# Turning the rows of a layer norm back with identity matmuls, outside the norms

## The chip, the cores and the metric

The kernel runs on one core of one Trainium2 chip. The time is what the device measures for one execution of the whole program, in microseconds (us). The engines are named as in the profile: PE (TensorE) multiplies matrices, PEld is its loading of weights, DVE (VectorE) and ACT (ScalarE) work element by element, POOL (GpSimd) issues the gathers, SP (SyncE) issues most loads.

## The reference

One decoder block on 512 tokens of width 2048, all in float32:

```
for l in range(DEPTH):                                            # DEPTH = 1
    h = hybrid_mixer(x, w_in[l], ..., w_out[l])                   # mLSTM and forgetting attention
    x = layer_norm(DN_ALPHA * x + h, ln_w[l, 0], ln_b[l, 0])      # norm 0
    h = memory_cross_attention(x, mem, w_xq[l], w_xkv[l], w_xo[l])
    x = layer_norm(DN_ALPHA * x + h, ln_w[l, 1], ln_b[l, 1])      # norm 1
    h = peer_ffn(x, peer_wq[l], peer_sub_keys[l], peer_u[l], peer_v[l])
    x = layer_norm(DN_ALPHA * x + h, ln_w[l, 2], ln_b[l, 2])
```

`layer_norm` takes off the mean over the 2048 columns, divides by the root of the variance plus 1e-5, multiplies by `w` and adds `b`. `peer_ffn` scores the tokens against sub-keys, selects 16 experts for each of 8 heads, multiplies the tokens by the experts' rows of `peer_u`, and sums rows of `peer_v` by the results.

## The kernel before, in words

**Matmuls in two parts.** Every large matmul is made of three matmuls in fp32r: a tile is split into a high part (rounded to fp32r by a copy on ACT, L157 for activations, L194 for weights) and a low part (the difference, on DVE, L158 and L199). High by high, high by low and low by high are summed. Weights come as 1 MB tiles `raw`; each is cast and subtracted into a **ring** tile of 4096 columns, half for the high and half for the low part. With one tile in the ring a raw tile is split in two shares that use the tile's halves in turn; `add_ring` adds a second tile, and from then on a whole raw tile is one share and the counter `ring["n"]` picks the tile:

```
L188  ring["n"] += 1
L190  t = ring["tiles"][ring["n"] % len(ring["tiles"])]
```

The first share after the second tile is added (before the output projections of blocks 1 to 3, at 2484 us) goes to the new tile, the next to the old one, `ring0`. `group_as` (L242) runs such shares with the activations as weights of PE and 512 columns moving: L262 and L263 for the high shares, L270 for the low one.

**Rows and columns.** The 512 tokens are four blocks of 128 rows. An object of class `Ends` holds one set of blocks: `e` block 0, `e1` block 1 (one block each), `e2` blocks 2 and 3. Each goes through a residual (L785: old rows times alpha plus the group's bank, for four groups of 512 columns), norm 0 (L802), the cross attention, a second residual and norm 1. A norm holds its rows in `r[t][g]` (block t, group g). Group by group it normalises the rows (L818 on ACT or L820 on DVE), turns them to columns by transposes (L828, with the 128x128 identity `ident` moving), applies scale and shift on the columns into `f` (L836 on ACT, L838 on DVE), and splits `f` into the high and low parts that the next matmuls take (L157, L158). Then it turns `f` back to rows: four transposes for each block and group into one bank (L852), a copy into `r[t][g]` on ACT (L853), and for the norms with `dst` a store to `x2d` in DRAM (L855). These rows are the next residual's old rows, and in DRAM the rows of `peer_ffn` and of the last residual. Over the six norms there are 32 such pairs of block and group.

**Order.** Python generators are mixed by hand (`mix`, `take`, `behind`), and the tile framework's scheduler orders each engine's instructions. Banks of PSUM: five `mm`, and three small ones in rotation (`sm_bank`: one `s1`, two `s2`). From norm 1 of `e2` on, products with the experts' rows for later use (`next_a`, L1388 to L1397, evacuated by L1402) run while the selection of experts for blocks 2 and 3 runs on DVE (L946 to L1009), and their bank `pa` is tagged `s2` too. Then the **gate build**: the chosen indices and gates are transposed (L1441), one-hot tiles are made (`o1` by L1455 with three buffers, `o0` by L1458), scaled on ACT (L1461), multiplied (L1462) and copied out (L1467), with a `next_a` after every second step.

## Time and profile before

| what | value |
|---|---|
| time, median of 3 runs | 4514.42 us (4506.16 to 4519.79) |
| the profiled execution's own time | 4513.31 us |
| its span, and TensorE clock granted | 4511.6 us, 0.991 |
| instructions | 65247 |
| PE, PEld, DVE, ACT, POOL busy | 98%, 88%, 83%, 49%, 20% |
| HBM over the span | 330 GB/s |

A row of a timeline gives an instruction's start, its duration, engine, line, operation, what is written and read, how many in a row, and in brackets the idle time of the engine before it and who ended it. A matmul's recorded duration overlaps the next one, so that what one costs in a stream is the distance between starts. A row of the table by stretches gives width, busy time of PE, PEld, DVE, ACT and POOL (with counts), the granted clock, the DMA engines' share and GB/s. The waits are grouped by the waiting line and its releaser: total, times, longest.

### The profile page before, as it was taken

To read this page: it belongs to the slowest core of one execution; us is meant where nothing else is said; L and a number is where in the kernel's file an instruction comes from. 1 tells how busy PE (TensorE), PEld (TensorE's weight loads), DVE (VectorE), ACT (ScalarE), POOL (GpSimd) and SP (SyncE) were. 2 spreads that over 40 slices of the span, in tenths; PEclk is the share of its full clock that TensorE was granted. 3 is DMA by queue.
4 is the path that set the end of the run, shared out by engine and by line. 5 is a ranking of instruction groups with operands and counts; after the bars stand their busy time and mean duration, and the time that the engine had idled before them with its cause. 6 is when DMAs were issued, how large, how long until landed. Compare 5 with 4: busy or idle time off the path is not lost.

```text
span 4511.6 us, 65247 instructions
## 1 busy us (share of the span) xinstructions
PE 4404.8 (98%) x25702; PEld 3956.5 (88%) x25702; DVE 3739.8 (83%) x4326; ACT 2229.7 (49%) x3032; POOL 896.6 (20%) x631
## 2 busy tenths in 40 slices
PE   9999999999999999999999999898999999999998
PEld 8888888889888899999999778898998778999996
DVE  7877767656899887888878778899988999889888
ACT  6876776645344432333333586543773444434443
POOL 1000000000133222322222000111222223334342
PEclk9999999999999999999999999999999999999999
DMA  8899989766798889898889876686989999999997
GB/s 313 316 328 339 335 322 339 277 225 216 264 345 335 338 339 351 336 345 320 325 336 353 299 255 233 266 326 246 361 351 421 418 421 410 383 393 391 390 365 304
DMA packets 246324, 1491.85 MB, mean 331 GB/s; under 512 B 26844, under 2 KB 54556, under 8 KB 77696
## 3 DMA queue, kind: packets, MB, share of 16 engines
q1 hardware_dynamic: 151680, 890.60, 52.4%
q0 software_dynamic: 81664, 561.95, 31.8%
q10 hardware_dynamic: 12672, 35.13, 2.0%
q8 instruction: 201, 3.29, 0.3%
q14 instruction: 107, 0.88, 0.1%
HBM read 1426.72 MB, written 60.86 MB: 330 GB/s over the span
## 4 chain that ended last, share of the span: by engine, by line
PE 63%; DVE 6%; issue 6%; DMA 3%; POOL 1%; ACT 1%; DVEq 0%; ACTq 0%; POOLq 0%
PE mm L220 22%; PE mm L270 6%; PE mm L262 6%; PE mm L263 6%; PE mm L1546 3%; PE mm L1547 3%; PE mm L1543 3%; PE pa L1396 3%; PE pa L1388 3%; PE pa L1391 3%; DVE ring L199 3%; DMA raw<-in_vD 2%; POOL rows L1067 1%; DVE rows L1087 1%; DMA rows<-in_peer_u,ei 1%
## 5 line engine op out<-in xcount | busy, mean ns | idle before, releaser
L194 ACT CAST ring<-raw 128x1024 fp32r<-128x1024 f32 x1568 | 1596.9, 1051 | 1456.4 <-PE mm L220 476.7
L199 DVE TENSOR_TENSOR ring<-raw,ring 128x2048 fp32r<-128x2048 f32 (+1 forms) x926 | 1811.5, 1960 | 509.8 <-ACT ring L194 250.6
L1067 POOL DMA_INDIRECT rows<-in_peer_u,ei x256 | 374.3, 1462 | 1588.9 <-DVE rows L1087 761.8
L220 PE MATMUL mm<-Ah,ring 128*128 128x384 f32 x2560 | 668.3, 339 | 1.8 <-ACT c L674 1.8
L1067 POOL DMA_INDIRECT rows<-in_peer_v,ei x256 | 455.5, 1779 | 926.4 <-DVE x2l L1103 608.1
L1103 DVE SCALAR_TENSOR_TENSOR x2l<-rows,dots,x2l 128x2048 f32<-128x2048 f32 x256 | 600.3, 2345 | 10.0 <-DMA rows<-in_peer_v,ei 9.8
L1087 DVE SCALAR_TENSOR_TENSOR rows<-rows,x2l 128x2048 f32<-128x2048 f32 x256 | 583.5, 2283 | 26.7 <-DMA rows<-in_peer_u,ei 26.4
L1391 PE MATMUL pa<-Xl,ring 128*128 128x256 f32 x2048 | 481.6, 279 | 0.0
L220 PEld LDWEIGHTS mm<-Ah,ring 128*128 128x128 f32 x2560 | 462.0, 188 | 8.0 <-ACT c L674 2.1
L220 PE MATMUL mm<-Al,ring 128*128 128x384 f32 x1280 | 427.0, 337 | 0.0
L1388 PE MATMUL pa<-Xh,ring 128*128 128x256 f32 x1792 | 421.9, 279 | 0.0
L1546 PE MATMUL mm<-ring,hph 128*128 128x512 f32 x1024 | 400.6, 393 | 8.3 <-ACT ring L194 6.3
L1547 PE MATMUL mm<-ring,hpl 128*128 128x512 f32 x1024 | 398.9, 391 | 0.1
L1391 PEld LDWEIGHTS pa<-Xl,ring 128*128 128x128 f32 x2048 | 387.2, 189 | 2.5
L1388 PEld LDWEIGHTS pa<-Xh,ring 128*128 128x128 f32 x1792 | 338.8, 189 | 0.1
L262 PE MATMUL mm<-ring,Zh 128*128 128x512 f32 x832 | 326.9, 393 | 3.2 <-ACT ring L194 3.2
L263 PE MATMUL mm<-ring,Zl 128*128 128x512 f32 x832 | 326.0, 392 | 0.0
L262 PE MATMUL mm<-ring,Ah 128*128 128x512 f32 x768 | 303.5, 395 | 1.1 <-ACT ring L194 1.1
L263 PE MATMUL mm<-ring,Al 128*128 128x512 f32 x768 | 300.1, 391 | 0.0
L220 PE MATMUL mm<-Bh,ring 128*128 128x384 f32 x1024 | 261.1, 337 | 0.6 <-DVE ring L199 0.6
L1543 PE MATMUL mm<-ring,hph 128*128 128x512 f32 x1024 | 254.4, 390 | 4.3 <-DVE ring L199 4.3
L220 PEld LDWEIGHTS mm<-Al,ring 128*128 128x128 f32 x1280 | 240.1, 188 | 3.2 <-issue 0.9
(405 smaller groups left out, 7230.1 us busy)
## 6 DMA issues: line engine op xcount, KB each, us to landing
raw<-in_w_in SPq DMA_DIRECT2D x256, 1024.0 KB
raw<-in_uT SPq DMA_DIRECT2D x128, 1024.0 KB
raw<-in_vD SPq DMA_DIRECT2D x128, 1024.0 KB
raw<-in_w_out SPq DMA_DIRECT2D x48, 1024.0 KB
raw<-in_peer_wq SPq DMA_DIRECT2D x48, 1024.0 KB
raw<-in_w_xkv SPq DMA_DIRECT2D x32, 1024.0 KB
raw<-in_w_br_ml SPq DMA_DIRECT2D x32, 1024.0 KB
raw<-in_w_br_fx SPq DMA_DIRECT2D x32, 1024.0 KB
```

What stands on the lines that cost most here:

```text
L194: x = nc.scalar.copy(hi[:, c:c + 1024], src[:, c:c + 1024])
L199: s = nc.vector.tensor_sub(lo, src, hi.bitcast(F32))
L220: i = nc.tensor.matmul(o, w, x, start=start and s % per == 0, stop=stop and s % per == per - 1)
L262: nc.tensor.matmul(banks[t], xh[:, tt], wh[:, c], start=k == 0, stop=False)
L263: nc.tensor.matmul(banks[t], xl[:, tt], wh[:, c], start=False, stop=False)
L1067: i = nc.gpsimd.indirect_dma_start(out=rows, out_offset=None, in_=I[table], in_offset=bass.IndirectOffsetOnAxis(ap=ei[t][:, k:k + 1], axis=0))
L1087: i = nc.vector.scalar_tensor_tensor(rows, rows, 1.0, tok[t]["x2l"], op0=ALU.mult, op1=ALU.mult, accum_out=d[:, k % GB:k % GB + 1])
L1103: i = nc.vector.scalar_tensor_tensor(acc, rows, d[:, GB + k % GB:GB + k % GB + 1], acc, op0=ALU.mult, op1=ALU.add)
L1388: i = nc.tensor.matmul(bank, uh[:, sl], xh, start=k == 0, stop=False)
L1391: nc.tensor.matmul(bank, uh[:, sl], xl, start=False, stop=False)
L1546: nc.tensor.matmul(banks[t][g], a[:, tt], vh[:, gs_], start=c == c0, stop=False)
L1547: nc.tensor.matmul(banks[t][g], b[:, tt], vh[:, gs_], start=False, stop=False)
```

## The change

The transposes back and their copies leave the norm. A new method `rows(t, g)` makes the same rows from the operand's two parts: eight matmuls of 128x128 for each block and group, with the high or the low part as weights and a rounded identity `identr` (fp32r) moving, summed in one small bank. For norm 0 the second residual calls it ahead of each group and copies the bank into `r[t][g]` (16 pairs in all). For norm 1, `rows_out` copies and stores them: for `e` and `e1` at the end of the norm, for `e2` (whose norm now has `dst` False) in the gate build, ahead of its first two `next_a`, into tiles with the tag `o1`. The identity is made in `gg[0]` and copied by ACT. And `ring["n"]` is advanced by one after the second ring tile is added, so that the first share goes to `ring0`.

```diff
-        ident = cp.tile([P, P], F32, tag="ident", name="ident")
-        make_identity(nc, ident)
+        gg = [cp.tile([P, P], F32, tag=f"gg{t}", name=f"gg{t}") for t in range(2)]
+        make_identity(nc, gg[0])
+        identr = cp.tile([P, P], F32R, tag="ident", name="ident")
+        nc.scalar.copy(identr, gg[0])
+        ident = identr.bitcast(F32)
...
+                    if not first:
+                        for t in range(nb):
+                            nc.scalar.copy(r[t][g], self.rows(t, g))
                     yield from group_as(W[g], X_, nb, ev)
 
+            def rows(self, t, g):
+
+                bank = sm_bank()
+                i = None
+                for c in range(4):
+                    for x in self.X[4 * g + c]:
+                        j = nc.tensor.matmul(bank[:, c * P:(c + 1) * P], x[:, t * P:(t + 1) * P], identr,
+                                             start=i is None, stop=c == 3 and i is not None and x is self.X[4 * g + c][1])
+                        if i is not None:
+                            after(j, i)
+                        i = i or j
+                return bank
+
+            def rows_out(self, pl):
+
+                for g in range(4):
+                    for t in range(self.nb):
+                        y = pl(t, g)
+                        nc.scalar.copy(y, self.rows(t, g))
+                        self.st.dma_start(x2d[self.b0 + t, :, g], y)
+
             def norm(self, i, o, alloc, dst, mid=None):
 
                 nb, r, sts = self.nb, self.r, self.sts
+                self.X = o
...
-                        fs.append(f)
-                    for t in range(nb):
-                        bank = sm_bank()
-                        for c in range(4):
-                            q = (c % cpb) * w + t * P
-                            nc.tensor.transpose(bank[:, c * P:(c + 1) * P], fs[c // cpb][:, q:q + P], ident)
-                        nc.scalar.copy(r[t][g], bank)
-                        if dst:
-                            self.st.dma_start(x2d[self.b0 + t, :, g], r[t][g])
+                if dst:
+                    self.rows_out(lambda t, g: r[t][g])
...
         add_ring(ctx.enter_context(pool("w2")))
+        ring["n"] += 1
...
-            e2.norm(1, X2, prX, True, mid)
+            e2.norm(1, X2, prX, False, mid)
...
             if t == 0:
+                e2.rows_out(lambda t, g: gp.tile([P, 512], F32, tag="o1", bufs=3, name=nm("xo")))
                 next_a()
                 next_a()
```

Three places show how the order moves; a line of the changed kernel has a number of its own (L199 becomes L201, L766 and L767 become L768 and L769, L836 becomes L862, L1461 becomes L1482).

**DVE at the output projections' start.** `ring_149` (before) and `ring_150` (changed) are `ring0`; `ring_19990` and `ring_20023` are the new tile. `raw_20002` and `raw_20035` are the first share, `raw_20019` and `raw_20052` the second. Before:

```order
L766 TENSOR_TENSOR sg_18385<-sg_18385,mm_19708 128x384
L199 TENSOR_TENSOR ring_149<-raw_20019,ring_149 128x2048
L767 TENSOR_TENSOR sg_18382<-sg_18382,m_2156_19949 128x384
L767 TENSOR_TENSOR sg_18383<-sg_18383,m_2159_19957 128x384
L767 TENSOR_TENSOR sg_18384<-sg_18384,m_2162_19965 128x384
L199 TENSOR_TENSOR ring_19990<-raw_20002,ring_19990 128x2048
```

The changed kernel:

```order
L768 TENSOR_TENSOR sg_18418<-sg_18418,mm_19741 128x384
L769 TENSOR_TENSOR sg_18415<-sg_18415,m_2156_19982 128x384
L769 TENSOR_TENSOR sg_18416<-sg_18416,m_2159_19990 128x384
L769 TENSOR_TENSOR sg_18417<-sg_18417,m_2162_19998 128x384
L201 TENSOR_TENSOR ring_150<-raw_20035,ring_150 128x2048
L201 TENSOR_TENSOR ring_20023<-raw_20052,ring_20023 128x2048
```

The first share's low part stood behind the second's; now it stands ahead of it, and directly behind the three L769.

**ACT in norm 1 of `e2`.** `f` is the scaled and shifted group, `Xh` a high part. Before, from the second pair of groups:

```order
L157 CAST Xh_22639<-f_22636 128x512
L836 ACTIVATE f_22664<-sm_22659,c_ln_bT,c_ln_wT 128x256 x2
L855 DMA x2d<-r_20270 128x512
L855 DMA x2d<-r_20275 128x512
L836 ACTIVATE f_22676<-sm_22671,c_ln_bT,c_ln_wT 128x256 x2
L157 CAST Xh_22667<-f_22664 128x512
L157 CAST Xh_22679<-f_22676 128x512
L853 COPY r_20546<-sm_22683 128x512
L853 COPY r_20551<-sm_22690 128x512
L836 ACTIVATE f_22704<-sm_22699,c_ln_bT,c_ln_wT 128x256 x2
L855 DMA x2d<-r_20546 128x512
L855 DMA x2d<-r_20551 128x512
```

The changed kernel:

```order
L159 CAST Xh_22736<-f_22733 128x512
L862 ACTIVATE f_22759<-sm_22754,c_ln_bT,c_ln_wT 128x256 x2
L159 CAST Xh_22750<-f_22747 128x512
L862 ACTIVATE f_22773<-sm_22768,c_ln_bT,c_ln_wT 128x256 x2
L159 CAST Xh_22762<-f_22759 128x512
L862 ACTIVATE f_22785<-sm_22780,c_ln_bT,c_ln_wT 128x256 x2
L159 CAST Xh_22776<-f_22773 128x512
```

The copies L853 and the stores L855 are gone from between the groups; nothing of other work has come in for them.

**ACT in the gate build.** The rows of the changed kernel behind the last evacuation of a `next_a` ahead of it (L1025 is the exponential of the gates, L825 and L826 the copies and stores of `rows_out`, L1482 the scaling of the one-hot tiles):

```order
L1025 ACTIVATE sel_g_22909<-sel_g_22909 128x256
L825 COPY xo_26011<-sm_26012 128x512
L825 COPY xo_26023<-sm_26024 128x512
L825 COPY xo_26035<-sm_26036 128x512
L826 DMA x2d<-xo_26011 128x512
L826 DMA x2d<-xo_26023 128x512
L826 DMA x2d<-xo_26035 128x512
L1482 ACTIVATE o_2853_26229<-o_2853_26229,gT 128x128 x4
L1482 ACTIVATE o_2856_26244<-o_2856_26244,gT 128x128 x4
L1482 ACTIVATE o_2863_26321<-o_2863_26321,gT 128x128 x2
L825 COPY xo_26047<-sm_26048 128x512
L1482 ACTIVATE o_2863_26321<-o_2863_26321,gT 128x128 x2
```

Before, the scalings followed the exponential directly. Now three of the eight copies stand between them, and the other five behind the tenth scaling and later.

**PE in the gate build.** Before, the last `next_a` ahead of the transposes and what follows:

```order
L1396 MATMUL pa_25970<-Xh_22759,ring_149 128x256 x2
L1397 MATMUL pa_25970<-X0h,ring_149 128x256
L1441 MATMUL mm_25963<-ident,sel_i_2556_22864 128x128
L1441 MATMUL mm_25963<-ident,sel_i_2558_22866 128x128
L1441 MATMUL mm_25963<-ident,sel_g_22868 128x128
L1462 MATMUL mm_26089<-o_2845_26092,o_2844_26090 128x128 x4
L1462 MATMUL mm_26104<-o_2848_26107,o_2847_26105 128x128 x4
L1388 MATMUL pa_26117<-X0h,ring_19990 128x256
```

In the changed kernel three pairs' matmuls of `rows` (L813, banks up to `sm_26036`) stand ahead of the transposes, the last of them shown here, and the other five pairs' behind them:

```order
L813 MATMUL sm_26036<-ident,Xh_22762 128x128
L813 MATMUL sm_26036<-ident,Xl_22763 128x128
L1461 MATMUL mm_26004<-ident,sel_i_2548_22905 128x128
L1461 MATMUL mm_26004<-ident,sel_i_2550_22907 128x128
L1461 MATMUL mm_26004<-ident,sel_g_22909 128x128
L813 MATMUL sm_26048<-ident,Xh_22750 128x128
L813 MATMUL sm_26048<-ident,Xl_22751 128x128
```

Behind these rows follow the rest of the five pairs, then two `next_a` (L1408 and on), and only then the first one-hot matmul (L1483); before, the last `next_a` stood ahead of the transposes.

More of the change, by code (lines that the diff above doesn't have):

```diff
@@ L149, in build @@
         cols = cp.tile([P, 2, TB, 4], F32, tag="cols", name="cols")
-        gg = [cp.tile([P, P], F32, tag=f"gg{t}", name=f"gg{t}") for t in range(2)]
         ticks = []
@@ L821, in norm @@
                                                     op0=ALU.subtract, op1=ALU.mult)
-                    fs = []
                     for cc in range(nb):
```

## The prediction

> **What bounds the kernel now.** I read the page's busy shares first, then PE's waits, then a table of the stretches that the edits touch, and last the timelines inside these.
>
> ```profile
> PE 4404.8 (98%) x25702; PEld 3956.5 (88%) x25702; DVE 3739.8 (83%) x4326; ACT 2229.7 (49%) x3032; POOL 896.6 (20%) x631
> ...
> PE mm L270 <- DVE ring L199: 14.0, 8, 4.7
> PE mm L1462 <- ACT o L1461: 9.4, 9, 6.2
> PE mm L1441 <- DVE sel_i L995: 7.7, 2, 4.3
> ...
> PE sm L852 <- ACT f L836: 5.0, 4, 1.7
> ...
> PE mm L1441 <- DVE sel_g L1009: 2.6, 1, 2.6
> ```
>
> PE is busy for 98% of the span, so work added to it costs its full length, except where PE idles. PE's longest waits lie exactly where the edits are: the ring (L270), the norms (L852) and the gate build (L1441, L1462). The next table tells stage by stage which case holds (width, then busy time of PE, PEld, DVE, ACT, POOL, the granted clock, DMA). Its rows are: `e`'s norm 0; the stretch behind it; `e`'s norm 1; the first output projection; `e1`'s norm 0; `e2`'s norm 0; `e1`'s norm 1; `e2`'s norm 1; the selection's end; the gate build.
>
> ```profile
> 816.00:850.00 34.00, 34.00 (x239) 31.33 (x238) 22.57 (x21) 22.90 (x32) 0.00 (x0) 1.00 0.65 230
> 890.00:960.00 70.00, 64.73 (x336) 57.30 (x335) 31.52 (x30) 32.20 (x47) 4.29 (x8) 0.93 0.53 189
> 1016.00:1040.00 24.00, 24.00 (x143) 22.65 (x142) 14.43 (x16) 17.38 (x29) 2.18 (x5) 1.00 0.62 217
> 2484.00:2500.00 16.00, 10.82 (x42) 8.41 (x41) 12.36 (x14) 8.60 (x10) 0.00 (x0) 0.89 0.84 307
> 2589.00:2616.00 27.00, 26.24 (x130) 21.13 (x129) 16.59 (x12) 21.46 (x37) 0.00 (x0) 1.00 0.69 242
> 2664.00:2697.00 33.00, 33.00 (x176) 27.68 (x174) 27.63 (x28) 29.15 (x45) 0.00 (x0) 1.00 0.79 277
> 2697.00:2722.00 25.00, 21.62 (x104) 16.47 (x103) 15.02 (x17) 24.40 (x51) 0.00 (x0) 0.94 0.56 187
> 2834.00:2869.00 35.00, 25.99 (x148) 21.86 (x149) 25.93 (x90) 26.18 (x46) 0.35 (x1) 0.76 0.49 171
> 3118.00:3148.00 30.00, 13.51 (x108) 12.55 (x106) 29.84 (x113) 5.00 (x12) 5.32 (x3) 0.79 0.50 190
> 3148.00:3300.00 152.00, 146.42 (x1212) 144.44 (x1213) 144.41 (x158) 118.05 (x308) 35.03 (x23) 0.99 0.88 343
> ```
>
> In `e`'s two norms and `e2`'s norm 0 PE never stops. In the norm 1 of `e1` and of `e2` it stands idle for 3.4 and 9.0 us, and the clock is down as well. At the selection's end it idles 16.5 us of 30 while DVE works 29.84.
>
> **The price of the rows.** Removed are 128 transposes L852, added are 256 matmuls of 128x128 in fp32r. What a transpose takes in a stream is read from L828, its twin of the same size:
>
> ```profile
> L852 PE MATMUL sm<-ident,f x128: 270/272/476, 821.1 to 2862.3; 128*128 128x128 f32 x128
> ...
> 1016.44 1.04 PE L828 MATMUL sm<-ident,r 128*128 128x128 f32 x8
> 1017.23 0.42 PE L220 MATMUL mm<-Ah,ring 128*128 128x384 f32 x1
> ```
>
> Eight in 0.79 us make 0.099 us each; scattered ones, each with a weight load that nothing overlaps, will be somewhat dearer, and I take 0.109. That is 128 x 0.109 = 14.0 us removed. A matmul with 128 weight columns and 128 moving ones in fp32r is not in the trace. Two kinds stand on either side of it:
>
> ```profile
> 1222.93 1.17 PE L631 MATMUL sm<-ones,p 128*128 128x1 f32 x10
> 1223.96 0.47 PE L262 MATMUL mm<-ring,Ah 128*128 128x512 f32 x1
> ...
> 26.93 0.22 PE L329 MATMUL sm<-Zh,gwh 128*68 128x128 f32 x1
> ...
> 29.91 0.34 PE L329 MATMUL sm<-gxh,gwh 128*68 128x384 f32 x1
> ...
> L631 PEld LDWEIGHTS sm<-ones,p x10: 188/192/192, 1222.7 to 1223.8; 128*128 128x128 f32 x10
> ...
> L330 PEld LDWEIGHTS sm<-Zl,gwh x16: 138/140/143, 26.9 to 29.7; 128*68 128x68 f32 x16
> ```
>
> L631 has the full 128 weight columns and one moving column: 1.03 us for ten, 0.103 each, although almost nothing moves, so the weight load sets the pace there. L329 to L331 have the 128 moving columns but only 68 weight columns: 48 matmuls in 2.98 us, 0.062 each. The new matmuls have L631's weight load and a little more to move. I take 0.112, with 0.062 and 0.115 as ends. 256 x 0.112 = 28.7 us, so PE gets 14.7 us more by the likely price and 1.9 by the low one.
>
> The Trainium skill ("TensorE: Matmul & The Clock Gate", section "Back-to-back issue gap") gives about 81 ns as the sustained spacing of matmuls with 128 moving columns and their weight loads. By it the 256 would take an estimated 20.7 us, 8 less than above. L631 with its 103 ns for a single moving column speaks against it for this type.
>
> **Stage by stage**, since a norm's waits can swallow this or give some back:
>
> *`e`, both norms.* PE has no gap, so the price counts in full: 64 x 0.112 − 32 x 0.109 = +3.7. The stretch behind norm 0 has 5.3 us of idle PE, and the first of its row matmuls may fall into it: −0.5. So +3.2.
>
> *`e1`, norm 0.* 32 x 0.112 − 16 x 0.109 = +1.8; of the 0.8 us idle most goes with the transposes that waited for `f`: +1.2.
>
> *`e2`, norm 0.* 64 − 32 of the same: +3.7. Eight copies less lie between the groups on ACT (29.15 of 33); I give that 1.7 back for the part of the norm that starts ahead of the row: +2.0.
>
> *`e1`, norm 1.* ACT, at 24.4 of 25 us, is the bound. Its four copies L853 go behind the norm's last group:
>
> ```profile
> L853 ACT COPY r<-sm x32: 572/587/660, 824.2 to 2863.0; 128x512 f32<-128x512 f32 x32
> ```
>
> 4 x 0.587 = 2.3 us come off the chain to the last high part, and the half of the clock's loss (0.06 x 25 = 1.5 us) 0.5 more; against it the 1.8 of PE work: −1.0.
>
> *`e2`, norm 1.* ACT again sets the end. The norm's chain and what it releases:
>
> ```profile
> 2843.69 0.58 ACT L1045 COPY sc<-sm 128x512 f32<-128x512 f32 x1 [2.16 <-PE sm L1043]
> ...
> 2853.28 1.07 ACT L853 COPY r<-sm 128x512 f32<-128x512 f32 x2 [1.93 <-PE sm L852]
> ...
> 2864.06 3.89 ACT L194 CAST ring<-raw 128x1024 fp32r<-128x1024 f32 x4
> ```
>
> From 2843.69 on ACT runs nearly without a gap to the ring cast that PE waits for. Eight copies, 8 x 0.587 = 4.7 us, go from this chain, and with them the 1.93 us that it stood for the transposes back: −6.6, say −6.5. The 32 transposes off PE lie inside this and aren't counted again; if PE becomes the end instead, the gain is those 3.5 us. A shorter idle also keeps the clock up (0.24 x 35 = 8.4 us lost now), which I leave for the range.
>
> *The ring's first share.*
>
> ```profile
> 2487.43 2.28 DVE L199 TENSOR_TENSOR ring<-raw,ring 128x2048 fp32r<-128x2048 f32 x1
> 2489.63 1.49 DVE L767 TENSOR_TENSOR sg<-sg,m 128x384 f32<-128x384 f32 x3
> 2491.04 2.28 DVE L199 TENSOR_TENSOR ring<-raw,ring 128x2048 fp32r<-128x2048 f32 x1
> ...
> 2493.38 1.83 PE L270 MATMUL mm<-ring,Ah 128*128 128x512 f32 x4 [4.04 <-DVE ring L199]
> ```
>
> The subtraction at 2487.43 is the second share's; PE waits for the one at 2491.04. Turned about, L767's three start at 2487.5, end at 2489.0, and the first share's low part is there 2.28 us later, at 2491.3 instead of 2493.3. With half of the clock's loss (0.11 x 16 = 1.8): −3.0. Its bounds are 0, if another cast comes late, and −5.2, the whole idle.
>
> *The gate build.* Here a wait is added.
>
> ```profile
> 3118.84 0.60 ACT L1402 ACTIVATE ga<-pa 128x512 f32<-128x512 f32 x1 [0.76 <-PE pa L1397]
> ...
> 3130.15 0.60 ACT L1402 ACTIVATE ga<-pa 128x512 f32<-128x512 f32 x1 [10.71 <-PE pa L1397]
> ...
> 3139.04 0.42 ACT L1006 ACTIVATE sel_g<-sel_g 128x256 f32<-128x256 f32 x1 [6.62 <-DVE sel_g L998]
> 3145.98 2.45 ACT L1461 ACTIVATE o<-o,gT 128x128 f32<-128x128 f32 x8 [6.52 <-DVE o L1458]
> ...
> 3134.43 0.33 PE L1441 MATMUL mm<-ident,sel_i 128*128 128x128 f32 x1 [4.32 <-DVE sel_i L995]
> ...
> 3147.89 3.76 PE L1462 MATMUL mm<-o,o 128*128 128x128 f32 x16 [6.21 <-ACT o L1461]
> ```
>
> From 3118.8 to 3130 PE runs two `next_a` (11.3 us) while DVE selects; then it only waits until 3147.89. In the changed order three pairs of rows take their place, and the two `next_a` stand behind all eight, in the same rotation of small banks. A pair's bank is free only after its copy on ACT, and ACT copies three pairs behind the exponential (from 3139.5) and the fourth behind ten scalings: 3145.98 + 10 x 0.306 = 3149.0. Pairs seven and eight need the banks of the fourth and fifth: their matmuls come at about 3150, the two `next_a` from 3151 to 3162, and the first one-hot product behind these: 14 us later than 3147.89. Behind it on PE's queue waits all of the gate build, and DVE waits too, since `o1` shares three buffers with the copies that are still to be stored. The 64 row matmuls themselves (7.2 us) fall into the idle time. The gate build's 5.6 idle us, which mostly come from DVE (144.41 of 152), can't take up more than a part of 14, as DVE is late by some 8 itself. I take +8.5; the ends are 0 (all made up later) and +14.
>
> *The start.* The identity's extra copy on ACT delays forty warm-up transposes that nothing waits for: 0.
>
> **Sum:** 3.2 + 1.2 + 2.0 − 1.0 − 6.5 − 3.0 + 8.5 = +4.4. The profiled execution took 4513.31, so 4517.7; the median of the runs shown is 1.1 above it, and I say 4518: no change that can be told, for about 0.3% (13.5 us) is what a measurement of this kernel can tell from none.
>
> **Rivals.**
>
> *Slower, 4535: the bank hold-up counts in full.* The rows' banks stop PE's queue in the gate build for 14 us, and the norms give back nothing but their transposes, because the next releaser (the table load and exponential of the other selection on ACT, PE's own queue) ends just behind the copies. Then the terms are 3.7 + 1.8 + 3.7 + 1.8 − 3.5 + 14 = +21.5. It decides when the first one-hot product starts more than 14 us behind the selection's end and PE's idle time up to 3300 stays at 5 us or more. For it: DVE is full for 152 us there. Against: `e2`'s norm 1 has 9.0 idle us.
>
> *Faster, 4500: the weight load isn't the limit.* At 0.062 each, `e`'s norms cost +0.5, `e1`'s 0.2 and 0.2 − 2.8, `e2`'s norm 0 0.5 − 1.7, `e2`'s norm 1 −8, the ring −4, and the delay in the gate build is made up but for 2: about −13. For it: L329's row. Against: its weights are barely half as wide, and L631's are not.
>
> *The clock, 4508.* A transpose may not count as work for the clock gate, a matmul by the identity does; the clock losses of the stretches at 890, 2697 and 2834 (4.9 + 1.5 + 8.4 = 14.8) would then go, some 10 more than I count. Against: 816 to 850 has as many transposes at 1.00, and the stretch at 2484 has none at 0.89. The Trainium skill (the same page, section "Part 4: PE-mode transpose") says that transposes don't count as busy for the clock; this rival is what that would make here, and the rows at 816 and 2484 disagree.
>
> **The numbers.** Forecast 0.55, slower rival 0.22, faster rival 0.17, the clock 0.06. The forecast's own range is 4506 to 4530 (gate build 0 to 14, the ring 0 to −5, matmuls 0.062 to 0.115 on the 192 that are on the path). Its tails and those of the rivals give faster 0.18, same 0.57, slower 0.25. The range of 8 in 10 takes in most of both rivals: 4499 to 4536.
>
> **What would show it.** Row matmuls about 0.11 us apart where PE is full (0.06: the faster rival). In the first projection L270 starts about 2 us earlier against the casts. `e2`'s norm 1 runs from `sc` to the ring cast in some 14 us instead of 20.4. The first one-hot product starts at least 10 us later behind the exponential than now (8.9 us). I am wrong if that distance hardly changes, if PE's idle time around the norms stays although the copies are gone, or if a stretch that no edit touches moves.

## The result

The changed kernel takes 4539.58 us (median of 6 runs, 4533.57 to 4552.19) where the kernel before takes 4513.49 (6 runs): a ratio of 1.006, with a 95% interval of 1.0048 to 1.0072. It is 26 us slower: above the range of 4499 to 4536, and twice the 13.5 us up to which the prediction would have called it no change. The time is near that of the slower rival, 4535; how far that was luck is said further down.

The profiled execution took 4548.83 us, 9 above the median of its own kernel, so its trace holds more loss than the typical run. Its page and its longest waits on PE:

```profile
span 4547.1 us, 65542 instructions
...
PE 4422.8 (97%) x25830; PEld 3979.4 (88%) x25830; DVE 3738.6 (82%) x4326; ACT 2229.4 (49%) x3033; POOL 873.3 (19%) x631
...
PE mm L1461 <- DVE sel_i L1014: 19.0, 2, 15.8
PE mm L272 <- DVE ring L201: 16.9, 10, 4.1
...
PE mm L1483 <- ACT o L1482: 7.7, 5, 3.3
...
PE sm L813 <- ACT Bh L159: 4.2, 1, 4.2
...
PE sm L813 <- ACT xo L825: 2.8, 1, 2.8
```

PE's busy time has grown by 18.0 us, 3.3 more than the 14.7 that the rows were priced at, and its share has fallen: work was added, and idle time too. The wait for the selection (L1461, L1441 before) has grown from 7.7 to 19.0 us, and two waits are new, L813 for a high part and L813 for a copy.

Since PE runs almost the same matmuls in both kernels, the difference between the starts of the same matmul in the two traces shows where the time went. From one point of the kernel before to the next this difference, called drift below, grew or fell by (us):

| stretch of the kernel before | what lies there | predicted | measured |
|---|---|---|---|
| 1000 to 1060 | `e`'s norm 1 | +1.8 | +1.7 |
| 2480 to 2512 | first shares of the ring | −3.0 | −2.4 |
| 2512 to 2530 | the shares behind them | 0 | +4.4 |
| 2585 to just ahead of 2702 | `e1`'s norm 0, `e2`'s norm 0 | with 2750 to 2842: +3.2 | −2.4 |
| 2702 to 2730 | `e1`'s norm 1 | −1.0 | +7.9 |
| 2750 to 2826 | `e2`'s second residual, with its rows | (above) | +8.9 |
| 2826 to 2842 | its end | (above) | −3.0 |
| 2842 to 2875 | `e2`'s norm 1 | −6.5 | −4.1 |
| 3110 to 3170 | selection's end, gate build | +14 | +15.7 |
| 3170 to 3450 | behind it | −5.5 | +9.5 |

Up to 800 us the profiles of the variants stand between 4.0 us ahead of that of the kernel before and 0.5 behind, and from 1640 to 1680 they lose between 0 and 9.6; neither goes with any edit, and both are left out. There is one profile of each kernel, so a stretch's drift by itself can hold an accident of one execution.

The rows' price came out as taken. The last two and three quarter pairs of `e1`'s norm 1 run in a row:

```profile
2725.49 0.28 PE L813 MATMUL sm<-ident,Bh 128*128 128x128 f32 x1
...
2727.84 0.27 PE L813 MATMUL sm<-ident,Bl 128*128 128x128 f32 x1
```

There are 21 steps between these starts, 0.112 us each. The Trainium skill ("TensorE: Matmul & The Clock Gate", section "Back-to-back issue gap") has 81 ns for 128 moving columns; for this type with 128 weight columns the trace disagrees.

The same stretches of the changed kernel, at their own times (columns as in the prediction): behind `e`'s norm 0, the first projection, `e1`'s norm 1, `e2`'s norm 1, the selection's end, the gate build.

```profile
905.00:975.00 70.00, 66.36 (x329) 59.86 (x329) 33.34 (x31) 35.43 (x50) 4.30 (x8) 0.98 0.66 249
2484.00:2500.00 16.00, 12.77 (x56) 10.55 (x55) 12.76 (x15) 9.16 (x11) 0.00 (x0) 0.89 0.95 344
2699.00:2732.00 33.00, 24.97 (x112) 20.78 (x111) 17.30 (x25) 24.03 (x48) 0.00 (x0) 0.79 0.46 158
2849.00:2880.00 31.00, 21.36 (x128) 19.41 (x128) 23.66 (x91) 21.88 (x37) 0.00 (x0) 0.78 0.36 136
3130.00:3178.00 48.00, 23.53 (x146) 22.61 (x146) 36.44 (x124) 12.62 (x25) 4.73 (x4) 0.64 0.45 170
3178.00:3330.00 152.00, 145.29 (x1213) 144.34 (x1212) 135.33 (x145) 107.65 (x275) 34.15 (x23) 0.97 0.92 351
```

In `e1`'s norm 1 PE now idles 8.0 us of 33 (3.4 of 25 before), at a clock of 0.79 instead of 0.94. Its longest wait there is for the first high part (`Bh`) of the norm. ACT's rows show why, first those of the kernel before, then those of the changed one, and last PE's wait:

```profile
2706.11 0.67 ACT L157 CAST Bh<-f 128x512 fp32r<-128x512 f32 x1
...
2708.81 1.28 ACT L869 ACT_TABLE_LOAD   x1
```

```profile
2708.80 1.28 ACT L888 ACT_TABLE_LOAD   x1
...
2717.62 1.73 ACT L159 CAST Bh<-f 128x512 fp32r<-128x512 f32 x3
...
2718.36 0.48 PE L813 MATMUL sm<-ident,Bh 128*128 128x128 f32 x1 [4.22 <-ACT Bh L159]
```

The table load belongs to the softmax of `e2`'s cross attention. Before, two high parts were cast ahead of it; now its exponentials (L888) and their scaling (L894) stand ahead of the first three. The fourth and last high part is cast no later than before (2721.5 and 2722.0). This is a place where the order moved that the description of the change doesn't list.

At the selection's end PE idles 24.5 of 48 at 0.64, and DVE, which was full there, idles 11.6 as well.

`e2`'s norm 1 does what the prediction said, from the copy of the scores to the ring's cast 14.7 us instead of 20.4:

```profile
2858.97 0.59 ACT L1064 COPY sc<-sm 128x512 f32<-128x512 f32 x1 [2.16 <-PE sm L1062]
...
2873.67 3.88 ACT L196 CAST ring<-raw 128x1024 fp32r<-128x1024 f32 x4
```

And the gate build, in the timelines of ACT, DVE and PE:

```profile
3151.07 0.42 ACT L1025 ACTIVATE sel_g<-sel_g 128x256 f32<-128x256 f32 x1 [19.92 <-DVE sel_g L1017]
3151.39 1.05 ACT L825 COPY xo<-sm 128x512 f32<-128x512 f32 x2
...
3158.01 3.03 ACT L1482 ACTIVATE o<-o,gT 128x128 f32<-128x128 f32 x10 [5.07 <-DVE o L1479]
3160.94 0.56 ACT L825 COPY xo<-sm 128x512 f32<-128x512 f32 x1
...
3165.27 0.59 ACT L825 COPY xo<-sm 128x512 f32<-128x512 f32 x1 [0.98 <-PE sm L813]
...
3165.62 0.69 DVE L1476 TENSOR_TENSOR o<-i1T,iota 128x512 f32<-128x512 f32 x1 [6.45 <-DMA x2d<-xo]
...
3146.46 0.48 PE L1461 MATMUL mm<-ident,sel_i 128*128 128x128 f32 x1 [15.82 <-DVE sel_i L1014]
...
3161.56 0.47 PE L813 MATMUL sm<-ident,Xh 128*128 128x128 f32 x1 [2.83 <-ACT xo L825]
...
3177.96 1.95 PE L1483 MATMUL mm<-o,o 128*128 128x128 f32 x16
```

From the exponential to the first one-hot product it takes 26.9 us, 8.9 before: 18 us more. Part of that is clock: behind the transposes the matmuls of `rows` run at steps of 0.213 us (21 steps from 3153.84 to 3158.32) instead of 0.112. ACT stands idle for 19.9 us ahead of the exponential and copies nothing, though the first banks of rows have been full since about 3130. The copies start right behind the exponential; DVE then waits 6.45 us for a store of `xo` before it may write `o1`.

### The profile page after: what moved, and what is told of

The parts are those of the page before. It is cut to its first block, busy times and chain, and to the rows that moved or that the text cites. A ratio compares the mean times of both kernels' runs of the same rounds, so it can differ in the third digit from the quotient of the medians.

```text
span 4547.1 us, 65542 instructions
## 1 busy us (share of the span) xinstructions
PE 4422.8 (97%) x25830; PEld 3979.4 (88%) x25830; DVE 3738.6 (82%) x4326; ACT 2229.4 (49%) x3033; POOL 873.3 (19%) x631
## 5 line engine op out<-in xcount | busy, mean ns | idle before, releaser
L201 DVE TENSOR_TENSOR ring<-raw,ring 128x2048 fp32r<-128x2048 f32 (+1 forms) x926 | 1811.1, 1960 | 541.6 <-ACT ring L196 276.0
L1086 POOL DMA_INDIRECT rows<-in_peer_u,ei x256 | 356.6, 1393 | 1643.0 <-DVE rows L1106 805.0
L1408 PE MATMUL pa<-Xh,ring 128*128 128x256 f32 x1792 | 421.2, 279 | 0.0
L1408 PEld LDWEIGHTS pa<-Xh,ring 128*128 128x128 f32 x1792 | 338.9, 189 | 0.1
```

The costliest lines, as they stand in the source:

```text
L201: s = nc.vector.tensor_sub(lo, src, hi.bitcast(F32))
L1086: i = nc.gpsimd.indirect_dma_start(out=rows, out_offset=None, in_=I[table], in_offset=bass.IndirectOffsetOnAxis(ap=ei[t][:, k:k + 1], axis=0))
L1408: i = nc.tensor.matmul(bank, uh[:, sl], xh, start=k == 0, stop=False)
```

## The experiments

All were timed against the kernel before on the same chip; drifts are against the one profile of before, in the stretches of the table above. Variants that turn some norms back as before use a switch in the changed kernel:

```diff
-            def norm(self, i, o, alloc, dst, mid=None):
+            def norm(self, i, o, alloc, dst, mid=None, turn=False):
...
-                self.X = o
+                self.X, self.turned = o, turn
...
+                        fs.append(f)
+                    for t in range(nb if turn else 0):
+                        bank = sm_bank()
+                        for c in range(4):
+                            q = (c % cpb) * w + t * P
+                            nc.tensor.transpose(bank[:, c * P:(c + 1) * P], fs[c // cpb][:, q:q + P], ident)
+                        nc.scalar.copy(r[t][g], bank)
+                        if dst:
+                            self.st.dma_start(x2d[self.b0 + t, :, g], r[t][g])
-                if dst:
+                if dst and not turn:
...
-                    if not first:
+                    if not first and not self.turned:
```

A norm called with `turn=True` makes its rows inside, by transposes, as before.

### The gate build

**Rows behind the two `next_a`** (rows_behind).

```diff
             if t == 0:
-                e2.rows_out(lambda t, g: gp.tile([P, 512], F32, tag="o1", bufs=3, name=nm("xo")))
                 next_a()
                 next_a()
+                e2.rows_out(lambda t, g: gp.tile([P, 512], F32, tag="o1", bufs=3, name=nm("xo")))
```

> The changed kernel with rows_out of e2 written behind the two next_a instead of ahead of them. In its order one pair of next_a stands ahead of the transposes again, as in the kernel before. The changed kernel runs 26.9 us from the exponential to the first one-hot product, the kernel before 8.9. Theory 1 (the two next_a on PE's queue behind the rows' banks are the hold-up): about 11 us come back, ratio to before 1.0035. Theory 2 (the copies, which wait for the selection's end because their tiles lie in the gate build's pool, and the one-hot tiles o1, which wait for the copies' stores, are the hold-up): little more than half of it comes back, since o1 still comes late; ratio 1.004 to 1.005, and DVE's wait for o1 is seen. Theory 3 (a delay there is made up later anyway): the ratio stays at 1.006.

Measured: 1.0038 (1.0025 to 1.005), 4536.33 us. About 10 us come back, in size what theory 1 says for PE's queue, and DVE's wait for `o1` is seen as theory 2 says:

```profile
3147.90 0.42 ACT L1025 ACTIVATE sel_g<-sel_g 128x256 f32<-128x256 f32 x1 [8.67 <-DVE sel_g L1017]
...
3168.25 0.69 DVE L1476 TENSOR_TENSOR o<-i1T,iota 128x512 f32<-128x512 f32 x1 [1.19 <-DMA x2d<-xo]
...
3159.70 0.47 PE L813 MATMUL sm<-ident,Xh 128*128 128x128 f32 x1 [4.14 <-ACT xo L825]
...
3169.83 1.05 PE L1483 MATMUL mm<-o,o 128*128 128x128 f32 x8
```

The first one-hot product still comes 21.9 us behind the exponential, but one `next_a` more is done by then than in the changed kernel. Theory 3, that the delay is made up later anyway, is out, since the ratio falls with the hold-up. The two others need the next run.

**Other tiles for the copies** (ga_tiles).

```diff
-                e2.rows_out(lambda t, g: gp.tile([P, 512], F32, tag="o1", bufs=3, name=nm("xo")))
+                e2.rows_out(lambda t, g: gap.tile([P, 512], F32, tag="ga", bufs=GA, name=nm("ga")))
```

> The changed kernel with the eight copies of e2's rows in tiles of the tag ga (seven of them, of an older pool) instead of o1. In its order all eight pairs of rows and the two next_a stand ahead of the transposes. Theory 2 (the tiles are the cause): the rows fall into PE's idle time of 15 us while DVE selects, the first one-hot product comes about 9 us behind the exponential as before, and the whole 18 us come back: ratio 1.002, about 4522. Theory 1 (only the small banks): the copies free the banks at once, so it says the same here; it differs from theory 2 in the run with the rows behind. Theory 3: no change, 1.006.

Measured: 1.0017 (1.0008 to 1.0026), 4523.62 us, as expected. Nothing but the tiles is edited. The order moves with them: all eight pairs of rows and the two `next_a` now stand ahead of the transposes, and the rows, the same matmuls and copies in the same small banks, run while DVE selects:

```profile
3134.09 0.58 ACT L825 COPY ga<-sm 128x512 f32<-128x512 f32 x1
...
3141.50 0.59 ACT L825 COPY ga<-sm 128x512 f32<-128x512 f32 x1 [0.94 <-DMA x2d<-ga]
...
3155.81 0.42 ACT L1025 ACTIVATE sel_g<-sel_g 128x256 f32<-128x256 f32 x1 [2.30 <-DVE sel_g L1017]
...
3164.67 3.57 PE L1483 MATMUL mm<-o,o 128*128 128x128 f32 x16 [6.21 <-ACT o L1482]
```

All eight copies end by 3142.1, ahead of the exponential, and the product comes 8.9 us behind it, as in the kernel before. The stretch 3110 to 3170 loses 0.7 us instead of 15.7, and 3170 to 3450 gains 0.2 instead of losing 9.5. So the choice of tiles, with the order that came of it, made the hold-up, and the small banks only passed it on: banks whose copies may run at once held up nothing here. That the copies had to wait because the `o1` tiles belong to a pool opened when the selection's own pool closes, and so lie where the selection still works, is how I read the program; shown is that tiles of an older pool don't wait.

**`e2`'s rows at the end of its norm** (e2_in_norm).

```diff
-            e2.norm(1, X2, prX, False, mid)
+            e2.norm(1, X2, prX, True, mid)
...
-                e2.rows_out(lambda t, g: gp.tile([P, 512], F32, tag="o1", bufs=3, name=nm("xo")))
```

> The changed kernel with e2's rows of norm 1 made and stored at the end of that norm, as for e and e1, and none in the gate build. Theory: the 18 us of the gate build go, and the norm gets 64 matmuls (7.2 us) and eight copies (4.7 us on ACT) back at its end, where PE waits for ACT: ratio 1.0035 to 1.004, about 4530. Rival (the rows at a norm's end run while PE would wait for the next ring casts anyway): 1.002. Rival (the gate build's delay isn't the loss): 1.006 or more.

Measured: 1.0029 (1.0019 to 1.0039), 4531.44 us, a little below the theory's 1.0035. The stretch 2842 to 2875 loses 6.0 us instead of gaining 4.1, and the gate build loses next to nothing (under 0.1). The last copy ends at 2878.9, and PE's next share waits for the ring:

```profile
2878.33 0.59 ACT L825 COPY r<-sm 128x512 f32<-128x512 f32 x1 [0.50 <-PE sm L813]
...
2884.01 1.99 ACT L196 CAST ring<-raw 128x1024 fp32r<-128x1024 f32 x2 [5.09 <-DMA raw<-in_peer_wq]
...
PE mm L222 <- ACT ring L196: 7.0, 1, 7.0
```

Taking the rows out of this norm is thus worth 10 us there; by the profiles the gate build and the stretch behind it took away 25 (15.7 and 9.5).

### The ring

**The ring's turn alone** (ring_only), in the kernel before:

```diff
         add_ring(ctx.enter_context(pool("w2")))
+        ring["n"] += 1
```

> The kernel before with the ring advanced by one, and nothing else. Theory (the prediction's term): the first low share comes 2 us earlier and half of the clock's loss there goes, 3 us faster than before, ratio 0.9993; in the profile PE's 4.0 us wait of the first L270 in the output projections is about 2 us shorter. Rival A: the gain is given back 30 us later, where the profile of the changed kernel has a 2.5 us wait and a half-clock stretch at 2516 to 2524 (5.3 us lost): then the ratio is 1.000 or a little over, and the same stretch is seen here. Rival B: that later loss is one execution's accident: then it is not in this profile.

Measured: 0.999 (0.9981 to 0.9999), 4515.11 us. The first low share comes earlier, 2.2 us up to 2512. But the stretch behind it loses 2.8, here and in every profile with the ring turned (4.4 in some). Of the stretch's two rows the first is of the kernel before, the second of the ring's turn alone:

```profile
2512.00:2536.00 24.00, 24.00 (x108) 19.87 (x107) 15.55 (x10) 13.24 (x13) 0.00 (x0) 1.00 0.79 296
```

```profile
2512.00:2536.00 24.00, 21.48 (x96) 17.44 (x95) 14.69 (x8) 11.70 (x12) 0.00 (x0) 1.00 0.72 281
...
2517.71 1.20 PE L270 MATMUL mm<-ring,Ah 128*128 128x512 f32 x4 [2.52 <-DVE ring L199]
```

A wait of 2.52 us for a later low share stands where PE didn't wait before. So rival A describes the trace: the wait has moved, not gone, and the two stretches all but cancel (+0.6 us). The time says 0 to 0.2% faster; where such a gain would come from stays open.

### The norms

**Norm 1 of `e2` alone** (tail_only), all else as before. This diff and those of the next runs are against the changed kernel; of a call that gets `turn=True` only the new line is shown:

```diff
+            e["x"].norm(0, X1, pr0, False, behind(ms, 2), turn=True)
...
+        e["x"].norm(1, X2, pr0, True, behind(ml, 1), turn=True)
...
-        ring["n"] += 1
...
+        e1.norm(0, X1b, pr1, False, behind(res, 2), turn=True)
...
+        e2.norm(0, X1c, lambda: pair(cpl, "X", 16), False, behind(res, 3, 2), turn=True)
...
+        e1.norm(1, X2b, pr1, True, behind(att, 2), turn=True)
...
-                e2.rows_out(lambda t, g: gp.tile([P, 512], F32, tag="o1", bufs=3, name=nm("xo")))
+                e2.rows_out(lambda t, g: gap.tile([P, 512], F32, tag="ga", bufs=GA, name=nm("ga")))
```

> The kernel before with one of the six norms changed: norm 1 of e2 gives up its transposes back, and its rows are made by the identity matmuls in the gate build, in tiles ga. All other norms turn back as before, and the ring isn't advanced. Theory: the norm gains the 4.2 us that the profile of ga_tiles shows between 2842 and 2875, and the rows cost 0.7 us in the idle of the gate build: 3.5 us faster, ratio 0.9992. Rival A: the 3.0 us gained from 2826 to 2842 belong to this norm too: 0.9986. Rival B: what the norm gains is given back by the experts' products behind it (the profiles show +2 at 2875 to 3080): 1.000.

Measured: 0.9997 (0.9988 to 1.0005), 4511.77 us. The norm gains 4.2 us again, and from 2875 to 3200 the trace loses 3.3 (where the ring's turn alone, which changes nothing there, is 2.9 ahead). That would be rival B, that what the norm gains is gone before the gate build ends. But the later profiles of tail_ring and norms1_of_e1_e2, which have the same edit, keep the gain: from 2875 to 3200 the first loses 0.9 and the second gains 0.4. So the loss in this one may be its own, and the time, with an interval that holds both 0.9992 and 1.000, can't tell the theory from rival B; only rival A, at 0.9986, lies outside it. **With the ring turned too** (tail_ring), against tail_only:

```diff
+        ring["n"] += 1
```

> As tail_only, with the ring advanced by one too. Theory: the ring's gain of 2.2 us at 2484 to 2512 is followed by a loss of 2.8 at 2512 to 2530 in every profile so far, so the ratio is that of tail_only within 0.0003. Rival (the time of the ring alone, 0.999, shows a real gain of 4 us): 0.001 below tail_only.

Measured: 0.9999 (0.9991 to 1.0008), 4513.95 us. The two together show no gain in time; a gain of 0.001 on top of tail_only isn't seen, nor quite excluded.

**The three norms 0 alone** (norm0_only):

```diff
+        e["x"].norm(1, X2, pr0, True, behind(ml, 1), turn=True)
...
-        ring["n"] += 1
...
+        e1.norm(1, X2b, pr1, True, behind(att, 2), turn=True)
...
-            e2.norm(1, X2, prX, False, mid)
+            e2.norm(1, X2, prX, True, mid, turn=True)
...
-                e2.rows_out(lambda t, g: gp.tile([P, 512], F32, tag="o1", bufs=3, name=nm("xo")))
```

> The kernel before with only the three norms 0 changed: their rows come from the identity matmuls ahead of each group of the second residual. Norms 1 turn back as before, the ring isn't advanced. Theory, from the stages of the profiles so far: about 0 for e, -0.8 for e1, -1.6 in e2's norm, +9.2 in e2's second residual (7.2 us of matmuls are expected there by price), -3.0 at its end: +4, ratio 1.0009. Rival (the +9.2 comes from e1's norm 1, whose end lies just ahead): then the stretch from 2750 to 2826 shows about +2 here, and the ratio is below 1.000.

Measured: 1.0009 (1.0 to 1.0018), 4520.55 us, the theory's number. The stretch 2750 to 2826 loses 8.4 us with norm 1 of `e1` unchanged, so this is in the main the rows' own: 64 matmuls at 0.112 are 7.2. From 2585 to 2702 it gains 2.5, as the changed kernel does (2.4), from 2826 to 2842 it gains 3.0, and `e1`'s norm 1, though not edited, loses 3.2.

**Norm 1 of `e1` alone** (e1n1_only):

```diff
+            e["x"].norm(0, X1, pr0, False, behind(ms, 2), turn=True)
...
+        e["x"].norm(1, X2, pr0, True, behind(ml, 1), turn=True)
...
-        ring["n"] += 1
...
+        e1.norm(0, X1b, pr1, False, behind(res, 2), turn=True)
...
+        e2.norm(0, X1c, lambda: pair(cpl, "X", 16), False, behind(res, 3, 2), turn=True)
...
-            e2.norm(1, X2, prX, False, mid)
+            e2.norm(1, X2, prX, True, mid, turn=True)
...
-                e2.rows_out(lambda t, g: gp.tile([P, 512], F32, tag="o1", bufs=3, name=nm("xo")))
```

> The kernel before with only e1's norm 1 changed: its four pairs of rows are made by identity matmuls at the end of that norm. Theory: the stretch from 2702 to 2730 loses 7.9 us as in the changed kernel, of which 1.8 are PE's added work and the rest PE standing behind the rows until the last group's high part is there (4.2 us) at half clock: ratio 1.0017. Rival (price alone): 1.0004. Rival (the loss comes from the rows of e2's norm 0, made nearby): no loss in that stretch here.

Measured: 0.9996 (0.9987 to 1.0005), 4511.48 us. Its stretch gains 2.4 us; I expected a loss of 7.9. So my reading of the changed kernel's trace was wrong: rows at the end of this norm don't cost it by themselves. The last rival is borne out so far that the loss needs something of a norm 0. The next three runs were to tell which.

**`e2`'s norm 0 put back** (e2n0_old), then **`e1`'s** (e1n0_old), each in the changed kernel with the tiles `ga`, to which these diffs are:

```diff
-        e2.norm(0, X1c, lambda: pair(cpl, "X", 16), False, behind(res, 3, 2))
+        e2.norm(0, X1c, lambda: pair(cpl, "X", 16), False, behind(res, 3, 2), turn=True)
```

> The changed kernel with the copies in tiles ga (as ga_tiles, which was 1.0017), and norm 0 of e2 turning back inside the norm as before; e's and e1's norms, norm 1 of e2 and the ring stay as changed. Theory: e2's norm 0 is what costs e1's norm 1 its cover, since with it PE is through the matmuls earlier that stood between the transposes. Then the stretch from 2702 to 2730 goes from +7.9 to about -2.4, the stretch from 2750 to 2826 from +9 to about 0, and the ratio is 1.0017 less 14 us: 0.9986. Rival (e1's own norm 0 takes the cover): the stretch from 2702 to 2730 stays near +8, only the e2 rows' price goes (some 4 us net), ratio 1.0007.

Measured: 1.003 (1.0018 to 1.0042), 4531.09 us: not faster than with it changed (1.0017, with an interval that overlaps this one), let alone at the 0.9986 expected. The stretch 2750 to 2826 falls to 4.0, but 2702 to 2730 loses 13.5 us. The theory fell, and its rival, with 8, is too small as well.

```diff
-            e1.norm(0, X1b, pr1, False, behind(res, 2))
+            e1.norm(0, X1b, pr1, False, behind(res, 2), turn=True)
```

> The changed kernel with the copies in tiles ga (1.0017), and only e1's norm 0 turning back inside the norm as before; e2's norm 0 is as changed. The run with e2's norm 0 put back told against my theory: the stretch from 2702 to 2730 lost 13.5 us there, more than the 7.9 of the changed kernel, so it isn't e2's norm 0 that takes the cover. New theory: it is e1's. Its rows are now made inside e1's second residual, whose last group (alpha times the old rows, on DVE, and the statistics) starts norm 1: with e2n0_old the copy of the last rows ends at 2712.1 and the statistics are joined at 2713.6, against 2694.7 before, some 10 us later than the drift up to there. So here the stretch should come back to about -2.4, as with e1's norm 1 alone, and the ratio to 0.9995 to 1.000. Rival (either norm 0 does it, by the PE work it adds): the stretch stays at +5 or more, ratio 1.001 or more.

Measured: 1.004 (1.0026 to 1.0053), 4530.99 us. The stretch 2702 to 2730 loses 8.5 us. This theory fell too: either norm 0 does it. (That the whole is slower than with `e1`'s norm 0 changed as well, 1.0017, isn't explained by this stretch and stays open.) Then **both norms of `e1`**, all else as before (e1n0_e1n1):

```diff
+            e["x"].norm(0, X1, pr0, False, behind(ms, 2), turn=True)
...
+        e["x"].norm(1, X2, pr0, True, behind(ml, 1), turn=True)
...
-        ring["n"] += 1
...
+        e2.norm(0, X1c, lambda: pair(cpl, "X", 16), False, behind(res, 3, 2), turn=True)
...
-            e2.norm(1, X2, prX, False, mid)
+            e2.norm(1, X2, prX, True, mid, turn=True)
...
-                e2.rows_out(lambda t, g: gp.tile([P, 512], F32, tag="o1", bufs=3, name=nm("xo")))
```

> The kernel before with both norms of e1 changed and nothing else. Norm 1 alone measured 0.9996 and -2.4 us in its stretch. New theory (the rows on the way to norm 1's start take its cover): the stretch from 2702 to 2730 loses 8 to 13 us, ratio 1.002 to 1.0028. Rival (a third part is needed too: the ring's turn or e's rows): the stretch stays near -2, ratio 0.9998.

Measured: 1.0032 (1.002 to 1.0044), 4527.57 us, and 14.0 us lost in the stretch: no third part is needed. The stretch 2695 to 2740 and PE's waits in it show the difference; first norm 1 alone, then both norms of `e1`, then `e1`'s norm 0 put back:

```profile
PE mm L272 <- DVE ring L201: 0.5, 1, 0.5
PE sm L813 <- ACT Bh L159: 0.4, 1, 0.4
...
2695.00:2740.00 45.00, 43.56 (x223) 35.88 (x222) 31.17 (x32) 40.09 (x70) 0.00 (x0) 1.00 0.66 234
```

```profile
PE sm L813 <- ACT Bh L159: 4.2, 1, 4.2
PE sm L855 <- ACT r L845: 3.4, 1, 3.4
PE sm L855 <- ACT f L863: 2.0, 1, 2.0
...
2695.00:2740.00 45.00, 34.69 (x158) 28.64 (x157) 23.16 (x29) 30.38 (x57) 0.00 (x0) 0.81 0.39 133
...
2699.36 0.69 DVE L799 SCALAR_TENSOR_TENSOR r<-r,mm 128x512 f32<-128x512 f32 x1 [0.80 <-ACT r L804]
```

```profile
PE sm L813 <- ACT Bh L159: 3.5, 1, 3.5
PE sm L855 <- ACT f L863: 2.5, 1, 2.5
PE mm L272 <- DVE ring L201: 2.5, 1, 2.5
...
2695.00:2740.00 45.00, 36.50 (x165) 30.16 (x164) 24.89 (x27) 31.02 (x55) 0.00 (x0) 0.85 0.53 185
```

In the first PE idles 1.4 us in all and the clock stays at 1.00; in the others it idles 8.5 to 10.3 us at 0.81 to 0.85. ACT's order goes with this in every profile. Where a norm 0 of `e1` or `e2` is changed, the first cast of `Bh` stands behind the other attention's table load, and the stretch loses: 3.2 us without norm 1 of `e1`, 7.8 to 14.0 with it, where PE waits 3.5 to 4.2 us for that cast. With norm 1 alone the cast stands ahead of the load (2709.39 and 2711.05), the wait is 0.4 us, and the stretch gains. What PE does in turn (start in us, kind and number in a row; "turn" is a transpose to columns, "back" one to rows, "rows" the identity matmuls, "mm" the large matmuls) tells why:

```
norm 1 alone                       e1's norm 0 put back
2692.25 back x4                    2679.32 mm x88
2692.69 turn x4                    2702.05 mm x8
2693.04 mm x23                     2704.61 turn x12
2698.36 turn x4                    2709.58 turn x4
...                                2713.79 rows x1
2703.96 mm x2                      2714.07 mm x1
2704.95 turn x8                    2714.60 rows x7
2705.85 mm x14                     2716.07 mm x11
2709.14 turn x4                    2720.64 rows x1
```

Where `e2`'s norm 0 still turns back, its transposes reach to 2703 and the large matmuls stand between the steps of both norms. With that norm shorter, 88 large matmuls run in one piece ahead of `e1`'s norm 1, and the norm's own chain through ACT, with the other attention's work in it, then lies bare. With `e1`'s norm 0 changed it is the norm's start that is late: its residual waits for the copy of the old rows (L804), which now stands on the way to the statistics. Both are read from the traces. That these two ways make the whole of the 8.5 and 14.0 us wasn't tried apart, and neither was ACT's order: no run changes where the first `Bh` stands and nothing else.

**The two harmless norms together** (norms1_of_e1_e2: norm 1 of `e1` and of `e2`, the latter in tiles `ga`):

```diff
+            e["x"].norm(0, X1, pr0, False, behind(ms, 2), turn=True)
...
+        e["x"].norm(1, X2, pr0, True, behind(ml, 1), turn=True)
...
-        ring["n"] += 1
...
+        e1.norm(0, X1b, pr1, False, behind(res, 2), turn=True)
...
+        e2.norm(0, X1c, lambda: pair(cpl, "X", 16), False, behind(res, 3, 2), turn=True)
...
-                e2.rows_out(lambda t, g: gp.tile([P, 512], F32, tag="o1", bufs=3, name=nm("xo")))
+                e2.rows_out(lambda t, g: gap.tile([P, 512], F32, tag="ga", bufs=GA, name=nm("ga")))
```

> The kernel before with the two norms 1 of e1 and e2 changed (e2's copies in tiles ga), all else as before. It joins the two parts that cost nothing alone (0.9996 and 0.9997). Theory: they add, -2.4 us at e1's norm and about -1 behind e2's, ratio 0.9993, which can't be told from 1 by much. Rival (each part's gain comes from the same slack, since both end in DVE-bound selections): 1.000.

Measured: 0.9991 (0.9981 to 1.0), 4511.22 us; the stretches gain 2.4 and 4.2 as alone. Its median is the lowest of all variants, 28 us below the changed kernel; by its interval it is at most just faster than the kernel before, and it can't be told from ring_only, tail_only or e1n1_only.

## Why the prediction was wrong, point by point

**The gate build: the mechanism right, the set-off wrong.** The hold-up was predicted at 14 us and measured at 18 from the exponential on, along the steps named, with PE waiting for a bank (2.83 us) and DVE for `o1` (6.45 us in the longest wait). The failed step is "I take +8.5", which let 5.5 of the 14 be made up behind. Nothing was made up: ga_tiles, free of the hold-up, has a ratio of 1.0017 against 1.006, so that the hold-up cost about 19 us (13 to 26 by the two intervals), all of it and not three fifths. That DVE, the bound up to 3300, was itself held up by `o1`, so that both bounds were late, is in the prediction, and would explain it; it is argued, not shown by a run of its own. And the prediction let the rows' copies stand behind the exponential because of the order it had; the run with other tiles and the same banks shows that the tiles put them there.

**`e1`'s norm 1: predicted −1.0, measured +7.9.** This is the second step that failed. The prediction took 2.3 us off ACT's chain to the last high part, with the rest of ACT's order as before. Alone the norm gains 2.4, so that holds for the norm by itself. In the changed kernel the order of ACT isn't as before: the first high part, not the last, comes 11.5 us later than before (2717.62 and 2706.11, with a drift of 1.4 ahead of the norm), behind the other attention's softmax, and PE stands for it (4.2 us) in a stretch with a clock of 0.79. Summing stage by stage, as if each stage kept its cover, missed this: it needs a norm 0 of `e1` or `e2` changed as well.

**Norms 0 of `e1` and `e2`: predicted +3.2, measured +3.5 without that loss** (−2.4, +8.9, −3.0). The price of 0.112 is confirmed by the starts; that the sum came out so near is partly luck, since the 3.0 us gained at the residual's end were not foreseen.

**`e2`'s norm 1: predicted −6.5, measured −4.1.** The chain on ACT got 5.7 us shorter (20.4 to 14.7) as worked out, within 0.8; PE then waits 4.2 us for the ring's cast instead of 2.6. In the kernel with nothing else changed the profile shows the 4.2 us gained lost again behind it, but two other profiles of the same edit keep them.

**The ring: predicted −3.0, measured −2.4 and then +4.4.** The first share was sized right (2.0 us worked out, from 2493.3 to 2491.3); the step that failed is the missing answer to what is late next. The stated bounds, 0 and −5.2, left out a loss.

**`e`: predicted +3.2.** Norm 1 gave +1.7 (1.85 by price). From 800 to 1000, around norm 0, the changed kernel gains 3.3 us, variants that leave `e` alone between −0.4 and 3.9: the rows of norm 0 cost nothing that can be told. I read this as the 5.3 us of idle PE behind it hiding more than the 0.5 I allowed.

**The rivals.** The slower rival counted the gate build in full, and that part came out: the first product starts 18 us later, and PE's idle time behind it was 6.7 us, above its limit of 5. That its 4535 lies so near 4540 is partly luck: it has +3.7 for `e`, of which the 1.7 of norm 1 was seen, 1.8 for `e1`'s norm 1, which lost 7.9, and 14 for the gate build, which cost about 19. The faster rival fell with the row of 0.112 us. The clock rival fell as well: the clock at 905 to 975 is 0.98 (0.93), but at `e1`'s norm 1 0.79 (0.94) and at `e2`'s 0.78 (0.76), with fewer transposes in both; in the first two it goes with PE's idle share, which is 5% there (8%) and 24% (14%), and in the third, with 31% (26%), it hardly moved. For the transposes as such the Trainium skill ("TensorE: Matmul & The Clock Gate", section "Part 4: PE-mode transpose") isn't borne out here; the last section has forty of them alone.

## What to carry to other kernels

When work is moved into another engine's idle time, ask of every tile it writes when it may be written, not only of its banks: the same copies cost about 19 us in tiles of a pool that opens late and next to nothing in those of an old one. Don't count on a delay being made up when the engine that bounds the stretch is delayed too; here none of it was. And a saving in one of two interleaved chains is not the chain's own: what it leaves early may have been the cover of the other, and the order on the engines that both share may change, so price the pair, and read the order of both.

## What was not expected of the hardware

The clock went down with the hold-up: at the selection's end the granted clock was 0.64 over 48 us with 24.5 us of idle PE, where it had been 0.79 over 30 us with 16.5. Whether the hold-up also cost something behind itself is open. The stretch 3170 to 3450 lost 9.5 us more (11.6 in rows_behind, −0.2 in ga_tiles), but variants without the hold-up lose up to 7.5 there (e1n0_old), and by the times the whole cost is 19 us, about the hold-up's own length. What grew in that stretch is mostly waiting: PE idles 16.1 us instead of 9.3, and its waits for scaled one-hot tiles (L1483, L1462 before) come to 7.7 us instead of 2.2.

Transposes alone seem to bring the clock up. At the start of the kernel before forty of them run with nothing else on PE (1.68 to 8.04 us); the number within a stretch stands in brackets behind PE's busy time:

```profile
1.70:5.20 3.50, 3.50 (x17) 3.50 (x18) 0.46 (x2) 0.40 (x1) 3.49 (x8) 1.00 0.94 328
5.30:8.00 2.70, 2.70 (x25) 2.50 (x23) 1.70 (x3) 2.18 (x4) 0.48 (x1) 1.00 0.88 348
```

They go from about 0.206 us each to 0.108, nearly the two spacings of the row matmuls above, 0.213 in the stretch with the lowered clock and 0.112 elsewhere. I read this as the clock coming up under transposes alone; the clock column, 1.00 in both stretches, doesn't show it.
